# Expert layer of a decoder: the order in which TensorE takes the matmuls of a large and a small expert

## The chip, the core and the metric

The kernel runs on one core of one Trainium2 chip. The metric is the device time of one execution in microseconds. The core's engines are named as in the profile: PE (TensorE, the matmuls; PEld are its weight loads), DVE (VectorE), ACT (ScalarE), POOL (GpSimd) and SP (SyncE, which issues nearly all DMAs here). They run side by side, each takes its own list of instructions in order, and semaphores order them among each other.

## The reference, cut to what matters

A decoder trunk of two layers on 256 tokens of width 1024, all in float32. Each layer has token mixers, then a feed-forward part; in the second layer this is a mixture of eight experts, and each token goes to its two best ones:

```
logits = t @ w_router                                   # (256, 8)
top_val, top_idx = top_k(logits, 2);  top_w = softmax(top_val)
combine = sum(one_hot(top_idx, 8) * top_w[..., None], axis=1)
for e in range(8):
    out += combine[:, e:e+1] * ((silu(t @ w1[e]) * (t @ w3[e])) @ w2[e])
```

Here w1 and w3 are 1024 x 3584 and w2 is 3584 x 1024 for each expert, so the expert weights are 352 MB in float32. The change touches only this loop.

## The kernel before

**Experts in pairs.** The router's result sorts the experts by their number of tokens. The four with most tokens are "large": each has 128 token slots. The other four are "small": each has 64. A large and a small expert make a pair, and four pairs are worked off. (A branch for experts with more tokens than slots follows; it is not taken with these inputs.) The hidden width of 3584 is cut into seven chunks of 512, so there are 4 x 7 = 28 steps, in `paired()`.

**Weights.** For each chunk an expert has six weight tiles of 1 MiB: two of w1, two of w3, two of w2. SP loads them into a ring of nine buffers, all named `raw` (`load_raw`, line 125); load number n waits until tile n - 9 has been used.

**Large expert.** Precision is kept by splitting each float32 operand in a high and a low part of the format fp32r, and adding three products (`mm3`, lines 154 to 158). ACT makes the high part `whi` (line 164), DVE the low part `wlo` (line 165), half a tile at a time, and then the raw tile is free. There are six buffers for each part. `up_large` takes four tiles and fills two PSUM tiles named `psu`, one for w1 and one for w3 (24 matmuls each); `gate_large` makes `gfm` from them (ACT line 872, DVE line 873); `turn_large` transposes it (`psT`, then `gTr` and `gTl`); `down_large` adds 24 matmuls into two PSUM tiles `psd` that live for the seven chunks.

**Small expert.** The matmuls take raw float32, with 64 token slots as stationary columns (128*64 in the profile's shapes). `up_small` (line 923) puts the w1 product into partitions 0 to 63 and the w3 product into 64 to 127 of one PSUM tile `psq`: 16 matmuls, alternating between the two. The profile has two records for each of these float32 matmuls, so 32. `gfs` and the transposes `psTs` and `gTs` follow, and `down_small` (line 944) adds 8 matmuls (16 records) into `psds`, again alternating between the two halves of the partitions. A raw tile of the small expert stays in the ring until PE has read it.

**Order.** The loop is software pipelined: step s does the large up of chunk s, the small up and the large down of chunk s - 1, and the small down of chunk s - 2. When a pair ends, its results are scattered to the tokens (`pssc`, added to `x`), and the next pair's inputs are gathered (`psg`). The order within each engine's list is set by a scheduler with a timeline of its own when the kernel is built; the text of the program is its starting point. `behind(ins)` (line 115) adds edges that make an instruction come after given ones in the list; the kernel before uses it for a few splits only.

Of the kernel before, what the change touches and what calls it, by code (L numbers as in the profile page):

```python
# [21 lines left out]
KD = D // P  # L22
# [73 lines left out]
def decoder_kernel(ctx, tc, x_in, consts_in, mconsts_in, bias_in, small_in, gln_in, gbs_in, norms_in, w_in,  # L96
                   w_br_a, w_br_b, w_br_c, w_br_d, w_gate, w_out, dense_w1, dense_w3, dense_w2,
                   router_in, moe_w, out):
    nc = tc.nc
# [14 lines left out]
    @contextmanager  # L114
    def behind(ins):
        with ExitStack() as st:
            for i in ins:
                st.enter_context(tc.issue_after(i.ins))
            yield
# [24 lines left out]
    def wsl(wt, k, c0, n):  # L144
        halves, ah = wt
        return tuple(p[:, k % ah, c0:c0 + n] for p in halves[k // ah])
# [4 lines left out]
    def w_rows(w, k0, nk, c0=0, n=D):  # L151
        return load_w(w[k0 * P:(k0 + nk) * P, c0:c0 + n].rearrange("(k p) n -> p k n", p=P), nk, n)

    def mm3(ps, lhs, rhs, start, stop):

        nc.tensor.matmul(ps, lhsT=lhs[0], rhs=rhs[0], start=start, stop=False)  # L156
        nc.tensor.matmul(ps, lhsT=lhs[0], rhs=rhs[1], start=False, stop=False)  # L157
        nc.tensor.matmul(ps, lhsT=lhs[1], rhs=rhs[0], start=False, stop=stop)  # L158

    def sl(pair, *idx):  # L160
        return (pair[0][idx], pair[1][idx])
# [452 lines left out]
    def out_proj(l, mT):  # L614

        ps = [[psB.tile([P, 512], F32, name=f"pso{t}{n}", tag="ax") for n in range(2)] for t in range(TT)]
        sqrt_table(mT[1].bitcast(F32)[:, KD - 1, 0:1])
        def part(i, wt, t):
            for k in range(2):
                for n in range(2):  # L620
                    mm3(ps[t][n], sl(mT, slice(None), 2 * i + k, slice(t * P, (t + 1) * P)),
                        wsl(wt, k, n * 512, 512), i == 0 and k == 0, i == 3 and k == 1)

        rows_by_token_tile(part, lambda i: w_rows(w_out[l], 2 * i, 2), 4)
        return ps
# [41 lines left out]
    def moe(i, norm_i, l, mT):  # L667
        with ExitStack() as lctx:
# [5 lines left out]
            ps = out_proj(l, mT)  # L674
# [179 lines left out]
            nch = FE // 512  # L854
# [5 lines left out]
                return w.rearrange("p (a n) -> p a n", a=a)  # L860


            def up_large(e, c, j0, xl):
                ps = psA.tile([P, 512], F32, name="psu", tag="mm")
                wt = [load_w(tile_of(e, c, j0 + j, 4), 4, 512) for j in range(2)]
                for k in range(KD):
                    mm3(ps, sl(xl, slice(None), k), wsl(wt[k // 4], k % 4, 0, 512), k == 0, k == KD - 1)
                return ps

            def gate_large(p1, p3):  # L870
# [14 lines left out]
            acc = {}  # L885

            def down_large(e, c, gT):
                if c == 0:
                    acc["l"] = [psB.tile([P, 512], F32, name=f"psd{n}", tag="ax") for n in range(2)]
                for j in range(2):  # L890
                    wt = load_w(tile_of(e, c, 4 + j, 2), 2, D)
                    for k in range(2):
                        for n in range(2):
                            mm3(acc["l"][n], sl(gT, slice(None), 2 * j + k), wsl(wt, k, n * 512, 512),
                                c == 0 and j == 0 and k == 0, c == nch - 1 and j == 1 and k == 1)

            def to_tokens(t, n, lhs, parts, w):
                ps = psA.tile([P, 512], F32, name="pssc", tag="mm")
# [16 lines left out]
            def up_small(e, c, xs):  # L915
                ps = psA.tile([P, 512], F32, name="psq", tag="mm")
                for j in range(2):
                    w1 = load_raw(tile_of(e, c, j, 4), 4, 512)
                    w3 = load_raw(tile_of(e, c, 2 + j, 4), 4, 512)
                    for k in range(4):  # L920
                        kk = 4 * j + k
                        for rows, w in ((LO, w1), (HI, w3)):
                            nc.tensor.matmul(ps[rows], lhsT=xs[:, kk], rhs=w[:, k], start=kk == 0, stop=kk == KD - 1)  # L923
                gf = wk.tile([P, 512], F32, name="gfs", tag="gfs", bufs=1)
                nc.scalar.activation(gf[HI], ps[LO], AF.Silu)  # L925
                nc.vector.tensor_tensor(out=gf[HI], in0=gf[HI], in1=ps[HI], op=ALU.mult)  # L926
                return gf
# [9 lines left out]
            def down_small(e, c, gT):  # L937
                if c == 0:
                    acc["s"] = psB.tile([P, 512], F32, name="psds", tag="ax")
                for j in range(2):  # L940
                    w = load_raw(tile_of(e, c, 4 + j, 2), 2, D)
                    for k in range(2):
                        for n, rows in enumerate((LO, HI)):
                            nc.tensor.matmul(acc["s"][rows], lhsT=gT[:, 2 * j + k], rhs=w[:, k, n * 512:(n + 1) * 512],  # L944
                                             start=c == 0 and j == 0 and k == 0, stop=c == nch - 1 and j == 1 and k == 1)

            def scatter_small(GT, w):
                ys = wk.tile([P, 2, 512], F32R, name="ys", tag="ys", bufs=1)
                split(ys[:, 0], ys[:, 1], acc["s"])
                for t in range(TT):  # L950
                    for n, rows in enumerate((LO, HI)):
                        to_tokens(t, n, GT[rows, 1, t], (ys[rows, 0], ys[rows, 1]), w[:, t])

            def paired():

                npair = NE // 2
                steps = npair * nch
                slots = {0: first}
                pend = gTs = None
                for s in range(steps + 1):  # L960
                    if s < steps:
                        pr, c = divmod(s, nch)
                        p1 = up_large(place_of[pr], c, 0, slots[pr].xl)
                    if pend is not None:
                        gT = turn_large(pend)
                    if s >= 2:
                        pr2, c2 = divmod(s - 2, nch)
                        down_small(place_of[npair + pr2], c2, gTs)
                        if c2 == nch - 1:
                            scatter_small(slots[pr2].GT, combp[:, :, npair + pr2:npair + pr2 + 1])  # L970
                    if s < steps:
                        gf = gate_large(p1, up_large(place_of[pr], c, 2, slots[pr].xl))
                        if c == nch - 1 and pr + 1 < npair:
                            nxt = slots[pr + 1] = Slots()
                            nxt.one_hot(None, posp[:, :, pr + 1:NE:npair])
                            nxt.inputs(0, NSLOT + NSMALL)
                            nxt.turned()
                    if s >= 1:
                        pr1, c1 = divmod(s - 1, nch)
                        gfs = up_small(place_of[npair + pr1], c1, slots[pr1].xs)  # L980
                        if s == steps:
                            sqrt_table(gfs[HI, 0:1], HI)
                        down_large(place_of[pr1], c1, gT)
                        if c1 == nch - 1:
                            scatter_large(slots[pr1].GT, combp[:, :, pr1:pr1 + 1])
                        gTs = turn_small(gfs)
                    pend = gf if s < steps else None
                down_small(place_of[NE - 1], nch - 1, gTs)
                scatter_small(slots[npair - 1].GT, combp[:, :, NE - 1:NE])

            def rest(first_slot):

                at = wk.tile([P, TT, NE], F32, name="at", tag="off", bufs=1)
                nc.vector.tensor_scalar(out=at, in0=beyond, scalar1=-float(first_slot), scalar2=None, op0=ALU.add)
                for e in range(NE):
                    sl_e = Slots()
                    nc.vector.memset(sl_e.G[:, :, 1].bitcast(F32), 0.0)
                    sl_e.one_hot(0, at[:, :, e:e + 1])
                    sl_e.inputs(0, NSLOT)
                    sl_e.turned()  # L1000
                    for c in range(nch):
                        p1 = up_large(e, c, 0, sl_e.xl)
                        gT = turn_large(gate_large(p1, up_large(e, c, 2, sl_e.xl)))
                        down_large(e, c, gT)
                    scatter_large(sl_e.GT, comb[:, :, e:e + 1])
# [8 lines left out]
            place_of = [0] + [nc.values_load(ixi[0:1, r:r + 1], engines=[mybir.EngineType.SP], min_val=0, max_val=NE - 1)  # L1014
                              for r in range(1, NE)]
            first.inputs(NSLOT, NSLOT + NSMALL)
            first.turned()
            with behind([marks["G"]]):
                comb, combp, cnt, beyond = weights(pm, place)
# [21 lines left out]
    ps = None  # L1041
    for l in range(DEPTH):
        mT = mixer_layer(l, norm_T(ps, 2 * l))
        if l % 2 == 0:
            ps = dense_ffn(l // 2, norm_T(out_proj(l, mT), 2 * l + 1))
# [56 lines left out]
```

## Time and profile before

| | |
|---|---|
| median of 3 runs | 1591.19 us (1590.26 to 1591.65) |
| profiled execution | 1589.84 us |
| its span, first to last instruction | 1588.1 us |
| mean granted PE clock | 0.988 |
| first psq to last psq block | 708.58 to 1555.37 us |

The page gives each engine's busy time over the span, the span in 40 slices, the DMA queues, the chain of work that ended last, and groups of instructions. Its averages run over stages with different limits; the part that the change touches is the stretch from about 683 us to 1577 us. Windows, timelines and waits are asked of the same execution. In a row of a group or a timeline, `out<-in` are the names of the tiles, `x` is a count, and square brackets hold the idle time of the engine before the row and what ended it. Ends of matmul records overlap the next starts, so that the pace of PE is read from starts.

### The profile page before, as it was taken

What the parts mean: (1) busy time and instruction counts of PE and PEld (TensorE: products, weight loads), DVE (VectorE), ACT (ScalarE), POOL (GpSimd) and SP (SyncE); (2) the same over time, 40 slices, a digit from 0 to 9 for tenths busy, and PEclk for the clock granted to TensorE, in tenths of its full rate; (3) what the DMA queues carried; (4) which work ended last, traced back from release to release, by engine and by line L of the source; (5) the groups of instructions that cost most, each with busy time, mean ns of one, the idle gap of its engine ahead of it and who ended that gap; (6) DMA issues with size and microseconds to landing.
All of it is one profiled execution on the core that took longest, in us unless ns stands there. A gap on an engine that the chain in (4) does not pass through costs nothing.

```text
span 1588.1 us, 20024 instructions
## 1 busy us (share of the span) xinstructions
PE 1531.3 (96%) x7508; PEld 1065.8 (67%) x7508; DVE 977.8 (62%) x1291; ACT 808.1 (51%) x1184; POOL 20.8 (1%) x47
## 2 busy tenths in 40 slices
PE   6999999999899999899999999999999999999997
PEld 5888897888788889776555555555555555555553
DVE  5896776665679777765445655454645554654444
ACT  5577746555464865554434534344434453444342
POOL 2000000000100000000000000000000000000000
PEclk9999999999999999989999999999999999999998
DMA  9565555555565645479998989999999999899993
GB/s 324 189 192 181 173 181 173 187 188 190 186 199 167 198 160 196 163 307 376 421 407 371 413 343 421 400 413 374 385 372 403 404 408 373 365 417 405 398 390 141
DMA packets 134890, 474.61 MB, mean 299 GB/s; under 512 B 7744, under 2 KB 77376, under 8 KB 91776
## 3 DMA queue, kind: packets, MB, share of 16 engines
q1 hardware_dynamic: 132512, 466.65, 76.2%
q0 software_dynamic: 1984, 6.08, 1.2%
q8 instruction: 61, 1.00, 0.3%
q10 hardware_dynamic: 288, 0.52, 0.1%
q14 instruction: 45, 0.37, 0.1%
HBM read 472.17 MB, written 1.05 MB: 298 GB/s over the span
## 4 chain that ended last, share of the span: by engine, by line
PE 89%; DVE 4%; ACT 4%; issue 2%; DMA 1%; SPq 0%; DVEq 0%; ACTq 0%
PE psw L240 16%; PE psq L923 14%; PE psw L242 8%; PE psu L157 7%; PE psu L158 7%; PE psu L156 6%; PE psds L944 5%; PE psd L157 3%; ACT whi L164 3%; PE psd L158 3%; DVE wlo L165 3%; PE psd L156 2%; PE psg L835 2%; PE psf L156 1%; PE psf L158 1%
## 5 line engine op out<-in xcount | busy, mean ns | idle before, releaser
L165 DVE TENSOR_TENSOR wlo<-raw,whi 128x1024 fp32r<-128x1024 f32 x546 | 647.7, 1221 | 252.8 <-ACT whi L164 249.6
L164 ACT ACTIVATE whi<-raw 128x1024 fp32r<-128x1024 f32 x546 | 554.0, 1053 | 130.4 <-PE psw L240 40.1
L240 PE MATMUL psw<-hp,whi 128*128 128x512 f32 x1088 | 388.6, 400 | 0.6 <-DVE hp L165 0.6
L242 PE MATMUL psw<-hp,wlo 128*128 128x256 f32 x1088 | 307.0, 282 | 0.0
L240 PEld LDWEIGHTS psw<-hp,whi 128*128 128x128 f32 x1088 | 205.1, 188 | 52.8 <-issue 3.3
L923 PE MATMUL psq<-raw,xs 128*64 128x512 f32 x896 | 218.6, 596 | 0.0
L242 PEld LDWEIGHTS psw<-hp,wlo 128*128 128x128 f32 x1088 | 206.3, 190 | 2.1 <-issue 1.1
L157 PE MATMUL psu<-wlo,xer 128*128 128x512 f32 x448 | 183.4, 409 | 9.5 <-DVE wlo L165 9.5
L156 PE MATMUL psu<-whi,xer 128*128 128x512 f32 x448 | 179.6, 401 | 1.3 <-DVE x L902 1.2
L158 PE MATMUL psu<-whi,xel 128*128 128x512 f32 x448 | 176.1, 393 | 0.0
L923 PEld LDWEIGHTS psq<-raw,xs 128*64 128x64 f32 x896 | 65.3, 137 | 129.0 <-issue 128.7
L925 ACT ACTIVATE gfs<-psq 64x512 f32<-64x512 f32 x28 | 16.5, 591 | 251.7 <-PE psq L923 251.7
L157 PEld LDWEIGHTS psu<-wlo,xer 128*128 128x128 f32 x448 | 84.6, 189 | 64.0 <-issue 30.0
L156 PEld LDWEIGHTS psu<-whi,xer 128*128 128x128 f32 x448 | 84.8, 189 | 41.9 <-ACT whi L164 17.0
L944 PE MATMUL psds<-raw,gTs 128*64 128x512 f32 x448 | 110.8, 604 | 0.0
L926 DVE TENSOR_TENSOR gfs<-gfs,psq 64x512 f32<-64x512 f32 x28 | 19.4, 692 | 137.7 <-ACT gfs L925 137.7
L158 PEld LDWEIGHTS psu<-whi,xel 128*128 128x128 f32 x448 | 84.8, 189 | 15.3
L157 PE MATMUL psd<-wlo,gTr 128*128 128x512 f32 x224 | 92.3, 412 | 2.1
L158 PE MATMUL psd<-whi,gTl 128*128 128x512 f32 x224 | 88.1, 393 | 0.0
L259 ACT ACTIVATE sum<-psw 128x256 f32<-128x256 f32 x120 | 44.8, 374 | 67.0 <-PE psw L242 67.0
L156 PE MATMUL psd<-whi,gTr 128*128 128x512 f32 x224 | 75.4, 413 | 2.7 <-ACT whi L164 2.7
L872 ACT ACTIVATE gfm<-psu 128x512 f32<-128x512 f32 x28 | 16.7, 597 | 119.9 <-PE psu L158 119.9
(260 smaller groups left out, 1570.4 us busy)
## 6 DMA issues: line engine op xcount, KB each, us to landing
raw<-in_moe_w_dram SPq DMA_DIRECT2D x336, 1024.0 KB, 8.2
raw<-in_dense_w_dram SPq DMA_DIRECT2D x33, 1024.0 KB, 5.3
raw<-in_w_gate_dram SPq DMA_DIRECT2D x32, 1024.0 KB, 5.4
raw<-in_w_in_dram SPq DMA_DIRECT2D x22, 1024.0 KB, 5.6
raw<-in_w_out_dram SPq DMA_DIRECT2D x8, 1024.0 KB, 5.0
raw<-in_w_br_c_dram SPq DMA_DIRECT2D x4, 1024.0 KB, 5.5
s<-in_bias_dram POOLq DMA_DIRECT2D x16, 192.0 KB, 4.2
gain<-in_norms_dram SPq DMA_DIRECT2D x5, 512.0 KB, 4.9
```

The lines of the kernel that those rows point to most:

```text
L156: nc.tensor.matmul(ps, lhsT=lhs[0], rhs=rhs[0], start=start, stop=False)
L157: nc.tensor.matmul(ps, lhsT=lhs[0], rhs=rhs[1], start=False, stop=False)
L158: nc.tensor.matmul(ps, lhsT=lhs[1], rhs=rhs[0], start=False, stop=stop)
L164: return (nc.scalar.activation(hi, src, AF.Copy), nc.vector.tensor_tensor(out=lo, in0=src, in1=hi.bitcast(F32), op=ALU.subtract))
L165: nc.vector.tensor_tensor(out=lo, in0=src, in1=hi.bitcast(F32), op=ALU.subtract))
L240: nc.tensor.matmul(ps.rearrange("p a t -> p (a t)"), lhsT=w[0], rhs=act[:, k].rearrange("p a t -> p (a t)"), start=start, stop=False)
L242: nc.tensor.matmul(ps[:, 1], lhsT=w[1], rhs=act[:, k, 0], start=False, stop=stop)
L259: nc.scalar.activation(out[:, b], ps[b][:, 1], AF.Copy)
L835: nc.tensor.matmul(ps[:, b, cs], lhsT=ht[part][:, t, k * P:(k + 1) * P], rhs=self.G[:, t].rearrange("p s n -> p (s n)")[:, cs], start=n == ...
L923: nc.tensor.matmul(ps[rows], lhsT=xs[:, kk], rhs=w[:, k], start=kk == 0, stop=kk == KD - 1)
L926: nc.vector.tensor_tensor(out=gf[HI], in0=gf[HI], in1=ps[HI], op=ALU.mult)
L944: nc.tensor.matmul(acc["s"][rows], lhsT=gT[:, 2 * j + k], rhs=w[:, k, n * 512:(n + 1) * 512], start=c == 0 and j == 0 and k == 0, stop=c = ...
```

## The change

Two things change in the expert loop. First, every matmul of `up_large`, `down_large`, `up_small` and `down_small` is put behind the one traced before it (`line["last"]`), so that the scheduler may no longer interleave these groups with each other. Transposes, gather and scatter matmuls get no such edge. Second, `down_small` moves in the program text from between the two halves of the large up to behind them. The order is now: large up (both halves), small down, small up, large down.

```diff
-    def mm3(ps, lhs, rhs, start, stop):
+    def mm3(ps, lhs, rhs, start, stop, after=()):
-        nc.tensor.matmul(ps, lhsT=lhs[0], rhs=rhs[0], start=start, stop=False)
+        with behind(after):
+            nc.tensor.matmul(ps, lhsT=lhs[0], rhs=rhs[0], start=start, stop=False)
         nc.tensor.matmul(ps, lhsT=lhs[0], rhs=rhs[1], start=False, stop=False)
-        nc.tensor.matmul(ps, lhsT=lhs[1], rhs=rhs[0], start=False, stop=stop)
+        return nc.tensor.matmul(ps, lhsT=lhs[1], rhs=rhs[0], start=False, stop=stop)
...
+            line = {"last": []}
...
 # up_large
-                    mm3(ps, sl(xl, slice(None), k), wsl(wt[k // 4], k % 4, 0, 512), k == 0, k == KD - 1)
+                    last = mm3(ps, sl(xl, slice(None), k), wsl(wt[k // 4], k % 4, 0, 512), k == 0, k == KD - 1,
+                               line["last"] if k == 0 else ())
+                line["last"] = [last]
...
 # down_large
-                            mm3(acc["l"][n], sl(gT, slice(None), 2 * j + k), wsl(wt, k, n * 512, 512),
-                                c == 0 and j == 0 and k == 0, c == nch - 1 and j == 1 and k == 1)
+                            last = mm3(acc["l"][n], sl(gT, slice(None), 2 * j + k), wsl(wt, k, n * 512, 512),
+                                       c == 0 and j == 0 and k == 0, c == nch - 1 and j == 1 and k == 1,
+                                       line["last"])
+                            line["last"] = [last]
...
 # up_small; down_small likewise
-                            nc.tensor.matmul(ps[rows], lhsT=xs[:, kk], rhs=w[:, k], start=kk == 0, stop=kk == KD - 1)
+                            with behind(line["last"]):
+                                line["last"] = [nc.tensor.matmul(ps[rows], lhsT=xs[:, kk], rhs=w[:, k], start=kk == 0,
+                                                                 stop=kk == KD - 1)]
...
 # paired()
-                    if s >= 2:
-                        pr2, c2 = divmod(s - 2, nch)
-                        down_small(place_of[npair + pr2], c2, gTs)
-                        if c2 == nch - 1:
-                            scatter_small(slots[pr2].GT, combp[:, :, npair + pr2:npair + pr2 + 1])
                     if s < steps:
                         gf = gate_large(p1, up_large(place_of[pr], c, 2, slots[pr].xl))
...
+                    if s >= 2:
+                        pr2, c2 = divmod(s - 2, nch)
+                        down_small(place_of[npair + pr2], c2, gTs)
+                        if c2 == nch - 1:
+                            scatter_small(slots[pr2].GT, combp[:, :, npair + pr2:npair + pr2 + 1])
                     if s >= 1:
```

What this does to the engines' lists is shown at three places. The first is PE before, in a step late in the fourth pair, around the small down (`psds`), which stands in two pieces between matmuls of the large up (`psu`); `x4` counts matmuls of the program.

```order
L156 MATMUL psu<-whi,xer 128x512
L944 MATMUL psds<-raw,gTs 64x512 x4
L157 MATMUL psu<-wlo,xer 128x512
L158 MATMUL psu<-whi,xel 128x512
L156 MATMUL psu<-whi,xer 128x512
L157 MATMUL psu<-wlo,xer 128x512
L158 MATMUL psu<-whi,xel 128x512
L944 MATMUL psds<-raw,gTs 64x512 x4
L156 MATMUL psu<-whi,xer 128x512
```

Later in the same step, still before the change, the small up (`psq`) is cut after its first matmul, and five of the large up stand in the gap; the large down (`psd`) follows.

```order
L156 MATMUL psu<-whi,xer 128x512
L923 MATMUL psq<-raw,xs 64x512
L157 MATMUL psu<-wlo,xer 128x512
L158 MATMUL psu<-whi,xel 128x512
L156 MATMUL psu<-whi,xer 128x512
L157 MATMUL psu<-wlo,xer 128x512
L158 MATMUL psu<-whi,xel 128x512
L923 MATMUL psq<-raw,xs 64x512 x15
L156 MATMUL psd_11115<-whi,gTr 128x512
```

In the changed kernel the same place of PE's list reads as follows (line numbers there are one higher in `mm3`, and eight to ten higher in the small matmuls).

```order
L157 MATMUL psu<-whi,xer 128x512
L158 MATMUL psu<-wlo,xer 128x512
L159 MATMUL psu<-whi,xel 128x512
L954 MATMUL psds<-raw,gTs 64x512 x8
L931 MATMUL psq<-raw,xs 64x512 x16
L157 MATMUL psd_11115<-whi,gTr 128x512
L158 MATMUL psd_11115<-wlo,gTr 128x512
L159 MATMUL psd_11115<-whi,gTl 128x512
```

The eight small-down and sixteen small-up matmuls now stand in one piece, after the whole large up and ahead of the large down. The last place is ACT from one `gfs` to the next, in a step of the fourth pair, before the change:

```order
L925 ACTIVATE gfs<-psq 64x512
L164 ACTIVATE whi<-raw 128x1024 x3
L934 ACTIVATE gTs<-psTs 128x256
L164 ACTIVATE whi<-raw 128x1024 x2
L164 ACTIVATE gTr<-psT 128x512
L164 ACTIVATE whi<-raw 128x1024 x2
L872 ACTIVATE gfm<-psu 128x512
L164 ACTIVATE whi<-raw 128x1024 x5
L925 ACTIVATE gfs<-psq 64x512
```

and with the change:

```order
L934 ACTIVATE gfs<-psq 64x512
L165 ACTIVATE whi<-raw 128x1024 x3
L943 ACTIVATE gTs<-psTs 128x256
L165 ACTIVATE whi<-raw 128x1024 x2
L165 ACTIVATE gTr<-psT 128x512
L165 ACTIVATE whi<-raw 128x1024 x4
L877 ACTIVATE gfm<-psu 128x512
L165 ACTIVATE whi<-raw 128x1024 x3
L934 ACTIVATE gfs<-psq 64x512
```

Two of the weight splits that stood behind `gfm` now stand ahead of it.

More of the change, by code (lines that the diff above doesn't have):

```diff
@@ L943, in down_small @@
                         for n, rows in enumerate((LO, HI)):
-                            nc.tensor.matmul(acc["s"][rows], lhsT=gT[:, 2 * j + k], rhs=w[:, k, n * 512:(n + 1) * 512],
-                                             start=c == 0 and j == 0 and k == 0, stop=c == nch - 1 and j == 1 and k == 1)
+                            with behind(line["last"]):
+                                line["last"] = [nc.tensor.matmul(
+                                    acc["s"][rows], lhsT=gT[:, 2 * j + k], rhs=w[:, k, n * 512:(n + 1) * 512],
+                                    start=c == 0 and j == 0 and k == 0, stop=c == nch - 1 and j == 1 and k == 1)]
             def scatter_small(GT, w):
@@ L991, in rest @@
             def rest(first_slot):
+                line["last"] = []
                 at = wk.tile([P, TT, NE], F32, name="at", tag="off", bufs=1)
```

## The prediction

> **What bounds the kernel now.** I read the page first, for the stage that counts and what is busy in it.
>
> ```profile
> span 1588.1 us, 20024 instructions
> PE 1531.3 (96%) x7508; PEld 1065.8 (67%) x7508; DVE 977.8 (62%) x1291; ACT 808.1 (51%) x1184; POOL 20.8 (1%) x47
> DMA  9565555555565645479998989999999999899993
> raw<-in_moe_w_dram SPq DMA_DIRECT2D x336, 1024.0 KB, 8.2
> ```
>
> PE is busy nearly always, and in the second half, the experts, the 16 DMA engines are too. So two candidates lie close together there, and neither the 96% nor the nines say which ends last. For that I cut the stage into steps at the first small up matmul (psq) of each chunk and asked for windows (columns: stretch, length, busy time of PE, its weight loads, DVE, ACT, POOL, then PE clock, DMA share, GB/s).
>
> ```profile
> 708.58:1555.37 846.79, 827.49 (x3566) 472.05 (x3567) 445.01 (x441) 371.62 (x456) 0.00 (x0) 1.00 0.96 394
> 1442.20:1473.84 31.64, 30.73 (x131) 17.07 (x130) 15.96 (x15) 13.65 (x16) 0.00 (x0) 1.00 0.98 401
> 708.58:737.02 28.44, 28.44 (x129) 17.38 (x128) 13.90 (x13) 11.38 (x13) 0.00 (x0) 1.00 1.01 415
> 737.02:762.77 25.75, 25.75 (x117) 15.02 (x117) 13.79 (x13) 11.86 (x14) 0.00 (x0) 1.00 0.87 352
> 711.60:743.20 31.60, 31.60 (x146) 18.50 (x144) 14.15 (x13) 12.33 (x14) 0.00 (x0) 1.00 0.89 359
> 743.20:774.80 31.60, 31.60 (x139) 18.29 (x136) 16.30 (x16) 14.81 (x18) 0.00 (x0) 1.00 1.02 423
> 1343.60:1375.20 31.60, 30.42 (x130) 16.79 (x129) 22.52 (x26) 15.95 (x20) 0.00 (x0) 1.00 1.01 415
> 1406.80:1438.40 31.60, 30.70 (x130) 17.05 (x129) 15.97 (x16) 13.54 (x16) 0.00 (x0) 1.00 1.00 414
> 1444.00:1448.00 4.00, 4.00 (x22) 1.40 (x19) 0.13 (x1) 0.00 (x0) 0.00 (x0) 1.00 0.76 248
> ```
>
> A full step takes 31.64 us. The first step of the stage does the same work in 28.44 us, and the order of its PE instructions is almost the one that the change prescribes: psq, large down, small down and each half of the large up run through undivided. So the new order stands priced in the old trace, once. A step loads twelve tiles of 1 MiB, 12.58 MB; at the best rate of the windows, 423 GB/s, that is 29.75 us, at 414 GB/s 30.4 us. In the 31.64 us step the rate is only 401, and the row 1444 to 1448 shows where it is lost: for about 4 us DMA falls to 248 GB/s, since SP stands before a ring buffer that PE has not released.
>
> ```profile
> 1438.92 6.45 SPq L125 DMA_DIRECT2D raw<-in_moe_w_dram  x2
> SPq L125 <- PE psq L923: 8.2, 4, 5.6
> ```
>
> SP's timeline: the first of the two issues is at 1438.92, the next one 6.1 us later. SP's waits from 1436 to 1468 (sum, times, longest): the longest is 5.6 us, for psq. Hence the loads are held up by PE, and PE sets the pace now; but only 1.2 to 1.9 us of a step separate it from the loads.
>
> **What the change does to PE's work in a step.** Nothing is added or removed: the same matmuls, loads and splits. Added edges are all from PE to PE, so they cost no wait on another engine; they only fix PE's order. It removes four cuts of a step, and these rows price them (PE's timeline: start, duration, instruction; I use differences of starts, since ends overlap).
>
> ```profile
> 1439.52 0.39 PE L156 MATMUL psu<-whi,xer 128*128 128x512 f32 x1
> 1439.84 1.07 PE L923 MATMUL psq<-raw,xs 128*64 128x512 f32 x2
> 1440.85 0.50 PE L157 MATMUL psu<-wlo,xer 128*128 128x512 f32 x1
> 1441.18 0.39 PE L158 MATMUL psu<-whi,xel 128*128 128x512 f32 x1
> 1441.41 0.39 PE L156 MATMUL psu<-whi,xer 128*128 128x512 f32 x1
> 1442.20 7.08 PE L923 MATMUL psq<-raw,xs 128*64 128x512 f32 x30
> ...
> 1460.95 1.94 PE L944 MATMUL psds<-raw,gTs 128*64 128x512 f32 x8
> 1462.82 0.50 PE L157 MATMUL psu<-wlo,xer 128*128 128x512 f32 x1
> 1463.16 0.40 PE L158 MATMUL psu<-whi,xel 128*128 128x512 f32 x1
> 1464.19 1.94 PE L944 MATMUL psds<-raw,gTs 128*64 128x512 f32 x8
> 1466.06 0.50 PE L156 MATMUL psu<-whi,xer 128*128 128x512 f32 x1
> 1467.15 0.50 PE L157 MATMUL psu<-wlo,xer 128*128 128x512 f32 x1 [0.59 <-DVE wlo L165]
> ...
> 708.58 7.09 PE L923 MATMUL psq<-raw,xs 128*64 128x512 f32 x32
> 727.78 3.65 PE L944 MATMUL psds<-raw,gTs 128*64 128x512 f32 x16
> 731.36 0.50 PE L156 MATMUL psu<-whi,xer 128*128 128x512 f32 x1
> ```
>
> 1. psq cut into 1 and 15 matmuls (2 and 30 records). The 30 records take 7.08 us and the undivided 32 take 7.09: the first matmul is free where its partner on the other 64 columns runs beside it, and costs 1440.85 − 1439.84 = 1.01 us where it stands alone. Entering costs 0.32 instead of the 0.23 between two psu (1441.18 to 1441.41), leaving again 0.33 instead of 0.23. Together 1.01 + 0.09 + 0.10 = 1.20 us.
> 2. psds cut into 4 and 4. Two blocks of 1462.82 − 1460.95 = 1.87 us are 3.74; undivided 731.36 − 727.78 = 3.58. With one crossing of 0.09 + 0.11 that is 0.16 + 0.20 = 0.36 us.
> 3. psds put directly ahead of psq: one crossing less, and the 0.1 us that a block of this kind needs to run out: 0.3 us.
>
> Sum 1.86 us. Fourth, a wait: the third large weight tile's low part comes late, 1467.15 − 1466.06 = 1.09 us between two matmuls of which 0.34 (as 1462.82 to 1463.16) are normal, so 0.75 us. Its cause stands on ACT and DVE:
>
> ```profile
> 1464.30 0.60 ACT L872 ACTIVATE gfm<-psu 128x512 f32<-128x512 f32 x1 [5.30 <-PE psu L158]
> 1464.79 3.89 ACT L164 ACTIVATE whi<-raw 128x1024 fp32r<-128x1024 f32 x4
> 1465.87 4.63 DVE L165 TENSOR_TENSOR wlo<-raw,whi 128x1024 fp32r<-128x1024 f32 x4 [5.43 <-ACT whi L164]
> ```
>
> ACT stands 5.30 us at gfm, which needs the first half of the large up; that half is stretched by a psds block in its middle, and the weight splits queue behind gfm. After the change two more splits stand ahead of gfm and no psds lies inside that half, so I take this wait as gone; bounds: 0 if another split is late instead, 0.75 if not. 31.64 − 1.86 − 0.75 = 29.0 us, against 28.44 measured for the one undivided step. I take 28.8 us of PE for a steady step.
>
> Over the stage, from the first psq to the last, 846.79 us: three turns from one pair of experts to the next, with gather and scatter work of their own, are four steps each,
>
> ```profile
> 826.98:958.32 131.34, 127.94 (x565) 74.64 (x564) 73.23 (x76) 59.26 (x76) 0.00 (x0) 1.00 0.92 376
> 1051.96:1184.11 132.15, 128.91 (x566) 74.75 (x565) 73.14 (x76) 59.38 (x76) 0.00 (x0) 1.00 0.92 379
> 1278.41:1408.23 129.82, 127.10 (x565) 74.55 (x564) 72.71 (x75) 58.03 (x75) 0.00 (x0) 1.00 0.94 386
> 1534.73:1555.37 20.64, 20.33 (x87) 9.26 (x88) 7.03 (x8) 5.71 (x8) 0.00 (x0) 1.00 0.93 385
> ```
>
> 393.31 us. Two of the four steps have the psq cut, three the psds cut: 2 × 1.20 + 3 × 0.36 + 4 × 0.3 = 4.7 us a turn, 14 in all, leaves 379. The two first steps stay (28.44 + 25.75 = 54.2), the last, short one is 20, and the other twelve become 12 × 28.8 = 346. **PE's sum: 799 us.**
>
> **What the loads allow.** 846.79 us at 394 GB/s are 333.6 MB, the same afterwards. At 423 GB/s they need 789 us, at 414 (a full window without a hole) 806. **So both limits fall together:** once PE needs only 28.8 us in a steady step, the 29.75 to 30.4 us of its loads are the longer. The turns need the reverse, about 31.6 us of PE a step, and there the ring of nine tiles can fill again, as the 376 to 386 GB/s of these rows show (loads held back). A lead of up to nine tiles evens the two out. I take the larger sum, 806, and 5 us more for the places where one limit hands over to the other: 811. That is 36 us less than 846.79. Ahead of the stage the order of every engine is unchanged, and the tail behind the last psq keeps its work.
>
> The profiled execution took 1589.84 us, 1.7 more than its span; the median of the runs is 1591.19, 1.35 above it. 1589.84 − 36 + 1.35 = **1555 us**. If PE's sum alone held, 847 − 799 = 48, it would be 1543.
>
> A page speaks against any gain. The Trainium skill, "DMA: Bandwidth & Descriptors", section Specifications, gives about 358 GB/s as the HBM limit of one core; 333.6 MB would then need 932 us, longer than the stage takes today. The windows above, 414 to 423 GB/s, contradict it, and "HBM Reference", section Specifications, says why: a core that streams alone measures near 425 (by that, 785 us).
>
> **Rivals.**
>
> *The loads gain only a little.* The hole in the loads moves instead of closing: a step's six small tiles stay in the ring until PE has used them, and the wait on psq becomes one on psds and psq together. Then the rate rises from 394 to about 403, half way to the full windows: 333.6 / 0.403 = 828, 19 us saved, 1572. For it: holes of that kind stand in rows that are otherwise undivided (359). Against it: in the undivided step the psds block lay a whole large-up half ahead of psq; in the new order the next release follows 3.5 us (half of 7.09) after it.
>
> *The rate does not rise at all.* 394 as now, 1591. What speaks for it is that DMA reads 0.98 already; against it, that the row of 0.98 contains the hole.
>
> *Undivided blocks starve the loads (slower).* In the two steps that are undivided already the rates are 415 and 352, over 54.19 us a mean of (28.44 × 415 + 25.75 × 352) / 54.19 = 385. PE could afford that with nine tiles in hand; if it holds for every step, 333.6 / 0.385 = 866, 20 us more, 1611. It decides as soon as the lasting rate falls below today's 394, that is when the hole of a step exceeds about 2 us more than 29.75. Against it: the very next window gives 423.
>
> *The order doesn't become what it says.* The new PE order does stand as blocks, only transposes and the gather (psT, psTs, psg) inside them, so this is not counted.
>
> **Chances and range.** Forecast (25 to 48 us less) 0.72; little gained 0.15; none 0.05; starved 0.08. The range 1543 to 1577 reaches from PE's sum to just past the first rival and leaves out 0.05 below and about 0.13 above. This kernel's runs lie within 0.1%, so 0.2% (3 us) is what can be told from no change: faster 0.87, same 0.05, slower 0.08.
>
> **What would show it.** Right: psq in 32 records of 7.1 us and psds in 16 of 3.6 everywhere, steady steps of 29.5 to 30.4 us, the 1.09 us gap gone, the stage at 410 GB/s or more and PE now waiting for splits whose tiles have just landed. The first term is wrong if psq takes 8 us though undivided; the load limit is wrong if steady steps come at 28.8 with the rate above 423; the whole is wrong if SP's longest wait per step stays near 6 us with the rate under 400.

## The result, and the profile after

The changed kernel takes 1544.17 us in the median (1543.0 to 1545.4), the kernel before 1591.42 (1590.26 to 1591.78) beside it. The ratio is 0.9704, 95% interval 0.9688 to 0.9721. That is 47.3 us less; 36 were forecast, and 48 where PE's sum alone holds. The time lies inside the range, but only 1 us above its lower end of 1543.

The page of the changed kernel; most of its lines answer to those shown of before:

```profile
span 1542.8 us, 20057 instructions
PE 1486.8 (96%) x7508; PEld 1072.2 (69%) x7508; DVE 979.9 (64%) x1291; ACT 809.6 (52%) x1184; POOL 20.3 (1%) x47
DMA  9656455555555555639999999999999999999994
L165 ACT ACTIVATE whi<-raw 128x1024 fp32r<-128x1024 f32 x546 | 554.6, 1054 | 272.8 <-DMA raw<-in_moe_w_dram 166.6
raw<-in_moe_w_dram SPq DMA_DIRECT2D x336, 1024.0 KB, 11.4
```

PE is as busy as before by share, 96%, with 44.5 us less. The nines of DMA now run without a gap through the second half. A load takes 11.4 us from issue to landing, 8.2 before: loads wait for each other in DMA instead of standing unissued on SP. And ACT now waits for landings, 166.6 us in all; before, it was 20.4 us (waits from 700 to 1550 us: sum, times, longest):

```profile
ACT whi L164 <- DMA raw<-in_moe_w_dram: 20.4, 11, 5.2
```

Windows of the changed kernel: the stage from the first small up to the last, two full steps, and the four steps around each turn (columns as before: PE, PEld, DVE, ACT, POOL busy, clock, DMA share, GB/s).

```profile
709.84:1510.24 800.40, 782.56 (x3565) 478.19 (x3566) 446.58 (x440) 371.50 (x454) 0.00 (x0) 1.00 1.00 413
1404.44:1433.77 29.33, 28.75 (x131) 17.29 (x128) 16.06 (x15) 13.65 (x16) 0.00 (x0) 1.00 1.02 421
1217.72:1246.14 28.42, 28.42 (x130) 17.32 (x128) 16.14 (x15) 13.77 (x16) 0.00 (x0) 1.00 1.01 420
823.22:948.67 125.45, 121.88 (x566) 75.38 (x564) 74.22 (x77) 60.61 (x77) 0.00 (x0) 1.00 1.00 412
1034.41:1159.64 125.23, 121.63 (x566) 75.51 (x564) 73.23 (x76) 60.31 (x77) 0.00 (x0) 1.00 1.00 416
1246.14:1375.12 128.98, 123.55 (x567) 75.50 (x565) 73.19 (x76) 60.56 (x77) 0.00 (x0) 1.00 0.97 400
```

The stage went from 846.79 to 800.40 us, 46.4 us, so nearly the whole gain lies there. The twelve steady steps take 28.1 to 29.3 us, 28.9 on average, instead of 31.6 on average; the three turns together take 379.7 instead of 393.3. PE is busy 44.9 us less in the stage (827.49 and 782.56), and idle nearly as long as before (19.3 and 17.8 us). Inside a step, PE's timeline:

```profile
1400.96 3.65 PE L954 MATMUL psds<-raw,gTs 128*64 128x512 f32 x16
1404.44 7.04 PE L931 MATMUL psq<-raw,xs 128*64 128x512 f32 x32
1411.41 0.50 PE L157 MATMUL psd<-whi,gTr 128*128 128x512 f32 x1
...
1413.28 0.50 PE L157 MATMUL psd<-whi,gTr 128*128 128x512 f32 x1 [0.21 <-ACT whi L165]
1413.71 0.46 PE L941 MATMUL psTs<-ident,gfs 64*128 64x64 f32 x4
1414.54 0.50 PE L158 MATMUL psd<-wlo,gTr 128*128 128x512 f32 x1 [0.37 <-DVE wlo L166]
```

The small down takes 3.48 us up to the small up, the small up 6.97 up to the large down. The 1.09 us gap in the large up is gone from the trace (16 of them before, none now). Grown is the wait in the last row: the large down stands before a low weight part behind psTs. Starts show 0.59 us from the last transpose to it, 13 times, where 0.15 are normal in undisturbed steps; before, 15 steps showed 0.36 there. What holds this part up stands in the lists of ACT and DVE:

```profile
1411.55 0.59 ACT L934 ACTIVATE gfs<-psq 64x512 f32<-64x512 f32 x1 [5.16 <-PE psq L931]
1412.17 2.96 ACT L165 ACTIVATE whi<-raw 128x1024 fp32r<-128x1024 f32 x3
1413.26 5.77 DVE L166 TENSOR_TENSOR wlo<-raw,whi 128x1024 fp32r<-128x1024 f32 x5 [0.39 <-ACT whi L165]
```

ACT stands 5.16 us at gfs, which needs the whole small up, and the split that PE will want is behind it in ACT's list, although its tile landed at 1407.7. In all 13 cases ACT stood at gfs (3.3 to 7.9 us) with the next tile landed 2.5 to 7.1 us before its split began. So the old gap, behind gfm, has a smaller successor behind gfs.

SP's waits, first before (1436 to 1468), then with the change (1404 to 1434): sum, times, longest, about a step each.

```profile
SPq L125 <- DVE wlo L165: 12.2, 6, 3.1
SPq L125 <- PE psds L944: 4.5, 2, 2.7
```

```profile
SPq L125 <- DVE wlo L166: 12.9, 6, 3.3
SPq L125 <- PE psds L954: 5.4, 3, 3.0
SPq L125 <- PE psq L931: 5.0, 2, 2.9
```

The longest wait for psq was 5.6 us before and is 2.9 now: tiles of the small expert come free close together, and in these steps the loads run at 420 to 421 GB/s. Holes remain in the turns (400 to 416 GB/s).

### The profile page after: what moved, and what is told of

It is laid out like the page before. It is cut to its first block, busy times and chain, and to the rows that moved or that the text cites. A ratio compares the mean times of both kernels' runs of the same rounds, so it can differ in the third digit from the quotient of the medians.

```text
span 1542.8 us, 20057 instructions
## 1 busy us (share of the span) xinstructions
PE 1486.8 (96%) x7508; PEld 1072.2 (69%) x7508; DVE 979.9 (64%) x1291; ACT 809.6 (52%) x1184; POOL 20.3 (1%) x47
## 4 chain that ended last, share of the span: by engine, by line
PE 92%; DVE 4%; ACT 2%; issue 1%; DMA 1%; SPq 0%; DVEq 0%; ACTq 0%
PE psw L241 17%; PE psq L931 13%; PE psw L243 8%; PE psu L158 7%; PE psu L157 7%; PE psu L159 7%; PE psds L954 7%; PE psd L158 3%; PE psd L157 3%; PE psd L159 3%; DVE wlo L166 2%; PE psg L836 2%; PE psf L157 1%; PE psf L159 1%; PE psf L158 1%; PE psb L157 1%
## 5 line engine op out<-in xcount | busy, mean ns | idle before, releaser
L165 ACT ACTIVATE whi<-raw 128x1024 fp32r<-128x1024 f32 x546 | 554.6, 1054 | 272.8 <-DMA raw<-in_moe_w_dram 166.6
L931 PE MATMUL psq<-raw,xs 128*64 128x512 f32 x896 | 198.1, 593 | 1.8 <-DVE x L909 1.8
L158 PE MATMUL psu<-wlo,xer 128*128 128x512 f32 x448 | 177.8, 397 | 0.0
L954 PE MATMUL psds<-raw,gTs 128*64 128x512 f32 x448 | 103.6, 599 | 0.0
L157 PE MATMUL psd<-whi,gTr 128*128 128x512 f32 x224 | 92.3, 412 | 2.7 <-ACT whi L165 2.7
L954 PEld LDWEIGHTS psds<-raw,gTs 128*64 128x64 f32 x448 | 29.8, 136 | 57.3 <-issue 56.3
## 6 DMA issues: line engine op xcount, KB each, us to landing
raw<-in_moe_w_dram SPq DMA_DIRECT2D x336, 1024.0 KB, 11.4
```

What stands on the lines that cost most here:

```text
L165: return (nc.scalar.activation(hi, src, AF.Copy), nc.vector.tensor_tensor(out=lo, in0=src, in1=hi.bitcast(F32), op=ALU.subtract))
L931: line["last"] = [nc.tensor.matmul(ps[rows], lhsT=xs[:, kk], rhs=w[:, k], start=kk == 0, stop=kk == KD - 1)]
L954: line["last"] = [nc.tensor.matmul(acc["s"][rows], lhsT=gT[:, 2 * j + k], rhs=w[:, k, n * 512:(n + 1) * 512], start=c == 0 and j == 0 and ...
```

## The experiments

**Theory:** PE's own time and its waits end the stage; the cuts cost what the rows of the prediction say; the loads keep up thanks to the ring. **Rival:** the loads end it, and the order of PE matters through the release of ring buffers. A third question is where the floor of the loads lies.

### One part at a time

The first kernel chains only the large up and the small up to each other; the small down stays free, and in its old place.

```diff
 # against the changed kernel
-                    if s >= 2:                 # small down behind the large up
-                        ...
+                    if s >= 2:                 # small down between its halves, as before
+                        ...
 # down_large, down_small: no edge
-                                       line["last"])
-                            line["last"] = [last]
```

> Edit: only the large up and the small up are chained to each other; the small and the large down are free and the small down stays between the two halves of the large up. The list has the small up in one piece of 16 everywhere (19 of 28 were cut 1 + 15 before) and the small down still in 4 + 4 in most steps. Theory (PE's own time sets the stage, loads keep up): 19 cuts x 1.20 us = 23 us less than the kernel before, about 1568; the 1.09 us gap before the low weight part stays. Rival (the loads set the pace, and the small down held in pieces keeps the hole in them): under 10 us less, above 1581.

Measured: 1568.52 us against 1590.19 (ratio 0.9868, 0.9852 to 0.9885), 21.7 us less. One step of it, as PE's timeline shows the small matmuls:

```profile
1423.10 7.09 PE L929 MATMUL psq<-raw,xs 128*64 128x512 f32 x32
...
1441.90 1.94 PE L951 MATMUL psds<-raw,gTs 128*64 128x512 f32 x8
1445.15 1.94 PE L951 MATMUL psds<-raw,gTs 128*64 128x512 f32 x8
```

Only the small up is whole here. 21.7 / 19 = 1.14 us a cut, 1.20 predicted. The rival, which expected under 10 us, falls: PE's time counts at once, though SP's longest waits for psq in this kernel are as long as before (10.4 us over the stage, both). PE's idle time in the stage is the same too, 19.9 us against 19.3.

The second kernel has all edges of the change, but the small down in its old place.

```diff
 # paired(), against the changed kernel
+                    if s >= 2:
+                        ...                    # small down (and its scatter)
                     if s < steps:
                         gf = gate_large(p1, up_large(place_of[pr], c, 2, slots[pr].xl))
...
-                    if s >= 2:
-                        ...                    # small down (and its scatter)
```

> Edit: all edges of the change, but the small down stays in the program between the two halves of the large up; it is one block of 8 there. Against the kernel before: 23 us for the small up, 24 small downs x 0.36 = 9 us, no adjoining of small down and small up; the gap before the low part may stay, since a block still stands in the large up. Theory: 1591 - 32 = 1559 with the gap, 1547 without it. Rival (what matters is that the small tiles are released close together): over 1575.

Measured: 1551.03 us (ratio 0.9756, 0.974 to 0.9772), between the two values of the theory, 17.5 less than the first kernel. The 1.09 us gap is gone here too (the profile has 16 such waits of 0.6 us, 9.5 in sum, before and in the first kernel, and none here), although the block still stands in the large up, between its halves. What is gone is the piece inside the first half, the half that gfm needs.

The third moves the small down in the program and adds no edge.

```diff
 # against the changed kernel: all four places
-                            with behind(line["last"]):
+                            with behind([]):
```

> Edit: the small down moves behind the large up in the program, no edge is added. The list then has the small up undivided already, but the small down still cut 4 + 4 around five large-up matmuls late in the large up. Theory: the changed kernel plus 0.36 + 0.3 us for about 20 steps, so 1544 + 13 = 1557. If the edges themselves do nothing beyond the list, and cuts of the small down are hidden behind waits for loads, 1544 to 1548.

Measured: 1553.6 us, scattered from 1551.72 to 1557.02 (ratio 0.9765, 0.9749 to 0.9782). The move alone makes the scheduler leave the small up whole; 9.4 us remain, for 23 small downs cut in two, 0.41 us each where 0.36 and up to 0.3 more were expected. This kernel does not have the 1.09 us gap either, and its pieces stand late in the second half; so the gap went with the piece in the first half, as the prediction has it. Each half of the change by itself brings most of the gain; they overlap in the largest term.

### What a cut costs

Two kernels cut the small up again, after its first or after its second matmul, and set the piece six large-up matmuls ahead of the end of the large up; a third has their order of loads and no cut.

```diff
 # up_large, second half
+                    if cut and k == KD - 3:
+                        line["last"] = [last]
+                        cut()                  # 1 or 2 matmuls of the small up; or only its loads
```

> Edit: the changed kernel, but the small up is cut after its first matmul, which is put six large-up matmuls ahead of the end of the large up (chained there). Theory of the pair (two matmuls on opposite 64 columns run beside each other; one alone wastes its slot): 27 cuts x 1.2 us = 32 us more than the changed kernel, 1576. Rival (a cut costs only the crossing, 0.3 us): 1552.

> Edit: as the cut after the first matmul, but after the second, so that both pieces have an even number. Theory of the pair: only the crossings are paid, 27 x 0.3 = 8 us, 1552. Rival (the cut itself costs 1.2 us, whatever its place): 1576, as with the odd cut.

> Edit: as the two cut kernels, with nothing cut: only the loads of the first two small-up tiles stand six large-up matmuls earlier in the program, so ahead of the two small-down tiles in SP's list. It asks what the cut kernels paid for the order of their loads. Odd cut 1584, even cut 1570, changed kernel 1544. If the order of the loads explains the even cut's excess over 0.3 us a step, about 1560. If the cut itself does, 1544.

Measured, one run each: 1584.43 after the first, 1570.05 after the second, 1547.95 without a cut. The order of the loads costs 3.8 us, not the 16 that would explain the even cut; and the even cut costs 22 us more than that, where the theory has 8. The two kernels' timelines show the price of a cut in a plain step, first the odd cut, then the even one:

```profile
1215.04 1.07 PE L934 MATMUL psq<-raw,xs 128*64 128x512 f32 x2
1217.63 3.65 PE L964 MATMUL psds<-raw,gTs 128*64 128x512 f32 x16
1221.12 7.04 PE L934 MATMUL psq<-raw,xs 128*64 128x512 f32 x30
```

```profile
1230.71 1.08 PE L934 MATMUL psq<-raw,xs 128*64 128x512 f32 x4
1231.72 0.50 PE L157 MATMUL psu<-whi,xer 128*128 128x512 f32 x1
1232.06 0.39 PE L158 MATMUL psu<-wlo,xer 128*128 128x512 f32 x1
...
1233.31 3.65 PE L964 MATMUL psds<-raw,gTs 128*64 128x512 f32 x16
1236.79 6.18 PE L934 MATMUL psq<-raw,xs 128*64 128x512 f32 x28
1242.90 0.50 PE L157 MATMUL psd<-whi,gTr 128*128 128x512 f32 x1
```

One matmul takes 1.07 us and two take 1.08; the other fifteen take 7.04, the other fourteen 6.18. So two matmuls on the two halves of the columns share a slot of 0.87 us (6.97 / 8), and an odd cut wastes one: this part of the theory holds. But the whole difference between the kernels is 14.4 us, not 27 x 0.86 = 23. For the even cut these rows give, by starts, 1.01 + 6.11 us where the undivided small up takes 6.97, and about 0.2 us for entering and leaving: 0.35 us a step, 9 us in all, not 22. Windows of the stage show more, without a cut, with the even and with the odd one:

```profile
708.10:1510.97 802.87, 783.38 (x3565) 478.94 (x3566) 448.42 (x440) 373.78 (x454) 0.00 (x0) 1.00 1.00 410
707.93:1535.71 827.78, 807.07 (x3572) 478.16 (x3572) 448.11 (x442) 371.86 (x455) 0.00 (x0) 1.00 0.97 400
709.06:1549.94 840.88, 825.48 (x3572) 484.57 (x3572) 448.97 (x442) 373.05 (x455) 0.00 (x0) 1.00 0.96 394
```

Against the kernel without a cut, PE is busy 23.7 us longer with the even cut, and idle only 1.2 us longer (20.7 against 19.5). So the even cut's cost lies in PE's own matmuls and not in waits for other engines. A part of it is seen at the turns, where scatter and gather matmuls break the small up again once it is cut, here into six matmuls, one and the rest (12 and 2 records are six matmuls and one):

```profile
1145.73 2.75 PE L934 MATMUL psq<-raw,xs 128*64 128x512 f32 x12
1148.40 0.74 PE L909 MATMUL pssc<-ys,GT 64*128 64x512 f32 x3
1149.07 1.07 PE L934 MATMUL psq<-raw,xs 128*64 128x512 f32 x2
```

Between the two cut kernels, PE is busy with the small up alone for 222.8 us with the odd cut, 202.8 with the even (190.2 without): 20 us, close to the theory's 23. In the whole time less of it is left, since PE is idle 15.4 us with the odd cut and 20.7 with the even one. How the remaining cost of the even cut divides was not separated.

### The floor of the loads

Two kernels leave out work of PE and no load: the product of the input's low part with the weights' high part, in both halves of the large up (16 matmuls of 0.23 us a step), or in the second alone (8).

```diff
 # up_large: mm3 without its third product
-                    last = mm3(ps, ...)
+                    nc.tensor.matmul(ps, lhsT=xl[0][:, k], rhs=wk2[0], start=k == 0, stop=False)
+                    last = nc.tensor.matmul(ps, lhsT=xl[0][:, k], rhs=wk2[1], start=False, stop=k == KD - 1)
```

> Edit: the changed kernel without the third product of the large up (low part of the input times high part of the weights): 16 matmuls of 0.23 us less in a step, so its output lacks that part. It asks where the loads' own limit lies. If the loads limit, the stage of 333.6 MB takes 333.6 / 0.421 = 792 us or a little more, 1536 to 1545, and PE waits in it. If PE alone limits, 28 x 16 x 0.23 = 103 us less, 1441.

> Edit: the changed kernel without the third product in the second half of the large up only (w3): 8 matmuls, 1.84 us less of PE in a step, 50 us in all, so its output lacks that part. If 1529, as without both, the loads end that run and the floor of the loads is there. If PE had still ended the other run, 15 / 103 of the PE time was seen and 1537 comes out here; if PE alone ended the changed kernel, 1494.

Measured, one run each: 1529.19 and 1533.43 us. 103 us less of PE's work bring 15, 50 us less bring 10.7. The second time lies between the 1529 and the 1537 of its expectation and does not decide by itself; the stage below does. Window and waits of the first of the two (waits: sum, times, longest):

```profile
702.07:1493.00 790.93, 734.28 (x3161) 403.37 (x3162) 450.97 (x445) 373.57 (x457) 0.00 (x0) 1.00 1.01 421
...
ACT whi L165 <- DMA raw<-in_moe_w_dram: 310.3, 35, 15.4
PE psq L933 <- DMA raw<-in_moe_w_dram: 16.1, 19, 1.4
```

Here PE itself waits for landings, and the rate stands at 421 GB/s over the whole stage. From the first psq to the last it takes 788 us, by starts. In the kernel with half the work left out the same stretch takes 787 us, again at 421 GB/s: twice the work taken from PE changes nothing there. That is the floor of the loads; the changed kernel's 800 us lie 12 above it. Not all of these 12 us could be won, since the time behind the last mark grew: from it to the end of the span are 37.2 us without the third product and 32.6 in the changed kernel.

### The ring

Two kernels give the ring of raw tiles seven or eight buffers instead of nine.

```diff
-NRAW_MOE = 5
+NRAW_MOE = 3                       # seven tiles; 4 for eight
```

> Edit: the changed kernel with a ring of seven raw tiles in place of nine. Theory (the ring's lead is what lets the loads run through while PE is at the turns and at the small blocks): holes come back in the loads, 10 to 40 us more, 1554 to 1584. Rival (three tiles under way are enough): within 3 us, 1541 to 1547.

> Edit: the changed kernel with a ring of eight raw tiles; seven gave 1557. Theory (the lead of the ring fills the turns and the blocks, and nine is just enough): between, 1546 to 1552. If the ring were still the limit at nine, half of seven's loss: 1550 or more.

Measured: 1557.07 with seven tiles and 1549.59 with eight, one run each; 1544.17 with nine. The time from the first psq to the last is 811.8, 801.0 and 800.4 us. Seven are too few, as the theory expects. Between eight and nine the stage hardly differs, but 4 of that pair's 5 us lie right behind the last mark, where with eight tiles the last small up waits for a load:

```profile
1511.10 4.45 PE L931 MATMUL psq<-raw,xs 128*64 128x512 f32 x18
1517.43 3.65 PE L931 MATMUL psq<-raw,xs 128*64 128x512 f32 x14 [1.88 <-DMA raw<-in_moe_w_dram]
```

With nine it runs through in 7.04 us. So eight fall short at the end of the stage and nine do not; more than nine were not tried, and 1549.59 lies so close to the 1550 of the second reading that the time alone does not decide between the two. The hand-over between the two limits, for which I had added 5 us, costs about nothing with nine.

### A try for more

```diff
 # paired(): scatter of the small expert
+                        with behind(line["last"]):      # after the next small up
+                            scatter_small(...)
```

> Edit: the changed kernel, but the scatter of a small expert at a turn is put behind the next small up, which needs nothing of it; PE waits about 1.3 us for the split of its sums and about 1 us more around it at each of three turns now. Theory (PE's own time and its waits at the turns set the end): 3 x 2 = 6 us less, 1538. Rival (the loads are the limit by now, the turns only let them catch up): no change, 1543 to 1545.

Measured: 1546.94 us (1546.58 to 1547.58; ratio 0.9728, 0.9712 to 0.9744), not better. The stage takes 801.0 us. In the changed kernel PE waits at a turn as these rows show, and in this one the waits come later:

```profile
918.26 0.74 PE L906 MATMUL pssc<-ys,GT 64*128 64x512 f32 x4 [0.70 <-ACT ys L165]
...
920.33 1.08 PE L931 MATMUL psq<-raw,xs 128*64 128x512 f32 x4 [0.61 <-DVE x L909]
```

```profile
929.50 0.51 PE L158 MATMUL psd<-wlo,gTr 128*128 128x512 f32 x1 [1.06 <-DVE wlo L166]
...
932.79 0.50 PE L158 MATMUL psd<-wlo,gTr 128*128 128x512 f32 x1 [0.65 <-DVE wlo L166]
```

The wait for the sums' split became a wait for weight splits of the large down, which now queue with the scatter's work on DVE. This differs from what was expected: the wait moved from the turn into the next large down, and the stage stands where it stood. PE is idle in it for 17.4 us, 17.8 in the changed kernel, so no gain was made that the loads could have taken. Neither the 1538 of the theory nor the rival's 1543 to 1545 came.

## Why the prediction was right, point by point

**What bounds it.** Right: PE set the pace, and the loads were held up by it. The first kernel shows it most plainly, since 1.14 us for each cut step went straight into the time.

**The terms.** They can be read off the series before, first, second, changed kernel: 21.7, 17.5 and 6.9 us. The second column takes the prediction's price of one cut times the number of cuts in the lists; it adds up to 52 us, while the prediction, which counted typical steps and turns, came to 48.

| term | predicted | measured |
|---|---|---|
| small up whole, 19 cuts | 23 | 21.7 |
| small down whole (9) and the gap (16 x 0.75 = 12) | 21 | 17.5 |
| small down next to small up, 27 x 0.3 | 8 | 6.9 |

In the second row the two parts are off in opposite directions, as the windows of the stage show in the first and the second kernel:

```profile
708.74:1532.80 824.06, 804.18 (x3565) 470.24 (x3566) 445.00 (x441) 371.88 (x456) 0.00 (x0) 1.00 0.98 404
709.15:1516.21 807.06, 790.25 (x3565) 475.78 (x3566) 445.87 (x440) 370.85 (x454) 0.00 (x0) 1.00 0.99 411
```

From the first to the second kernel PE is busy 13.9 us less in the stage (804.18 and 790.25) where 9 were priced, and idle only 3.1 us less (19.9 and 16.8) where the gap was to give 12. The prediction had set this as the bound of that term, "0 if another split is late instead": the gap went, and longer waits behind psTs and new ones at the turns took most of its place. The last row compares medians from two sets of runs.

**PE's sum.** 799 us predicted, 800.4 measured, and its parts agree too: 379 and 379.7 for the turns, 28.8 and 28.9 for a steady step. That it fits so well is in part luck. Of its 48 us some 39 were to come from the cuts and 9 from the gap; the windows show 44.9 us less of busy time and 1.5 us less of idle time. The cuts cost more than their price, and nearly all that the gap gave went to other waits.

**The loads: the step that failed.** I took the larger of the two sums, "806, and 5 us more for the places where one limit hands over to the other". The mechanism stood (after the change the two limits are close, 788 and 799), but this term was mis-sized by 11 us: 800 instead of 811, and so 1555 instead of 1544. Two things in it were wrong. The 414 GB/s came from windows in which PE was still the limit, and a window at 423 stood beside it; 421 is what the loads do when asked, and at that rate 333.6 MB take 792 us, less than PE's sum. And the hand-over costs nothing: steady steps of 28.9 us are shorter than the 29.9 that their loads take at 421 GB/s, so they live on the lead that the ring gained in the turns. With seven tiles, where this lead is smaller, the stage takes 811.8 us.

**The rivals.** Little gained and starved loads both rested on the hole that stays; SP's longest wait for psq fell to 2.9 us in a step (from 700 to 1500 us, SP waited 224 us for psq before and 145 with the change), and the rate is 413. Neither came. Without the third product the loads moved 421 GB/s over 791 us. The Trainium skill, "DMA: Bandwidth & Descriptors", section Specifications, gives about 358 GB/s as the HBM limit of one core; the 421 measured here do not agree with that. The Trainium skill, "HBM Reference", section Specifications (TRN2), gives about 425 GB/s for a core that streams alone; the 421 come close to it.

**The signs.** psq in 32 records of 7.0 us, psds in 16 of 3.65 (two of the 28 small downs, one at a turn and the last one, are still cut), the gap gone, the rate above 410: as said. Steady steps were to be 29.5 to 30.4 us; they are 28.1 to 29.3. That is one half of the sign that the load limit is wrong; the other half, a rate above 423, did not come (421). One sign failed: PE was to wait for splits "whose tiles have just landed". It waits for splits, but their tiles had landed 2.5 to 7.1 us earlier, and ACT came late from gfs.

## What to carry to other kernels

A stage whose old trace holds one step in the new order already prices the change: look for the odd step out, at its start or end, before adding up small costs. Matmuls that share a slot on two halves of the columns should be kept in even numbers, and blocks of different kinds whole, since each cut costs at once where PE sets the pace. After such a change, look for the next instruction that stands in its engine's list ahead of work that is ready: here PE's wait for the split behind gfm went, and the one for the split behind gfs grew. For the other limit, take the rate from a stretch where that limit acts, or leave out work until it does; a rate read while something else limits is only a lower bound.

## What was not expected

The even cut cost 22 us over the kernel without a cut, where the rows of a plain step account for 9; the rest is PE's own matmuls too, not waits, and is explained only in part. The time ahead of the stage, which no edit touches, differs between single profiles: the first matmul of the large up starts at 683.4 us in one and at 686.5 us in another. That is as large as the 2.8 us by which the late scatter lost, so this loss is not explained.
